# Expert feed-forward layer: the weights, not the tokens, held in the TensorE array

## The chip, the cores and the metric

The kernel runs on one core of a Trainium2 chip. The metric is device time in microseconds (us), lower is better. A run of the kernel before took 1444.42 us (median of three, 1442.44 to 1445.25). A profile of one execution gives for each engine what it did and when: TensorE (PE for matmuls, PEld for its loads of the stationary operand), VectorE (DVE), ScalarE (ACT), GpSimd (POOL) and SyncE (SP, whose queue issues the large loads).

## The reference

A two-layer decoder trunk on 256 tokens of 1024 channels, in float32. Each layer has a token mixer and a feed-forward part; the second layer's feed-forward part is a mixture of experts, and it alone is changed:

```
logits = h @ w_router                      # h: RMS-normed, 256 x 1024; 8 experts
top_vals, top_idx = top_k(logits, 2)       # each token goes to two experts
gates = softmax(top_vals)
for each expert e, on the tokens sent to it:
    y = (silu(x @ w_gate[e]) * (x @ w_up[e])) @ w_down[e]    # 1024 -> 3584 -> 1024
out[token] += gate * y
```

All eight experts together have 3 x 8 x 1024 x 3584 weights, 352 MB in float32, and every one is read once. With these inputs no expert gets more than 87 tokens.

## The kernel before, in words

A TensorE matmul holds a stationary operand (`lhsT`, up to 128 columns) in the array and streams a moving operand (`rhs`) past it; the result has one row per stationary column and lands in PSUM. A float32 matmul of the program is carried out as two load-and-stream pairs, so the profile counts two matmuls and two loads for each. The array can be used as four tiles of 32 columns each, which hold different operands and stream at the same time; which tile is meant is set by the output's start partition (0, 32, 64 or 96).

Tokens are gathered per expert (`fetch`, L969): a one-hot matrix of up to 96 columns (`CAP`) picks an expert's tokens out of `hn` by a matmul and leaves them in `xe`, channels on partitions. Tokens are the stationary operand. In `lanes` (L992 to L1003) the 96 tokens fill three of the four 32-column tiles, and 512 columns of the weights stream past (L998); the fourth tile takes the first 32 tokens of the next 512 weight columns (L999). The other 64 tokens of those columns are done in a second PSUM bank with 256 weight columns at a time (L1003). So each slice of 128 input channels and 1024 weight columns (a "k-step" below) takes two rounds of 512 columns and two of 256, four tiles at once, the pairs of passes counted.

`mm_in` runs eight k-steps for the gate or the up projection of 1024 hidden channels, `mm_down` four for half of that. A step `s` of the main loop (28 in all) is: gate, the rest of a finished expert if there is one, `turn`, the gather for a coming expert, up, and two `mm_down` for the step before. `turn` (L1030) transposes the 96 x 1024 hidden activations, since they come out with tokens on partitions and have to go in with channels there. `scales` (L983) fetches the gates and the norm factors per token, which `swi` and `y_evac` apply as per-partition scalars. `back` (L1070) and `scatter` (L1085) put a finished expert's output back to its tokens by one-hot matmuls and add it to `xt`.

TensorE's order is written out by hand in this stage. The weights come through a ring of nine 2 MB buffers: `Stream.done` (L216) issues the next load on SP's queue when the matmuls on a buffer have ended, so the loads run up to nine buffers ahead. At the end one branch (L1256) skips code for experts with more than `CAP` tokens.

Of the kernel before, what the change touches and what calls it, by code (L numbers as in the profile page):

```python
# [15 lines left out]
P = 128  # L16
T = 256
# [15 lines left out]
CAP = 96  # L33
# [4 lines left out]
def hybrid_decoder(  # L38
# [810 lines left out]
    hn = big.tile([P, 2, D], F32, tag="x3", name="hn")  # L849
    lps = bank("C")  # L850
# [33 lines left out]
    def sm2(name):  # L884
# [25 lines left out]
                             op0=OP.mult, op1=OP.add)  # L910
    region.close()


    io = moe.tile([P, 2, P], F32, name="io", bufs=1)
    for b, c0, n, pat, base in ((0, 0, 96, [[1, 96]], 0), (0, 96, 32, [[1, 32]], 0), (1, 0, 128, [[0, 2], [1, 64]], 32)):
        POOL.iota(io[:, b, c0:c0 + n], pattern=pat, base=base - BIG, channel_multiplier=0,
                  allow_small_or_imprecise_dtypes=True)
    lane = moe.tile([P, 3], F32, name="lane", bufs=1)
    DVE.memset(lane, 0.0)
    DVE.memset(lane[96:128, 0:1], 1.0)  # L920
    DVE.memset(lane[0:64, 1:2], 1.0)
    DVE.memset(lane[64:128, 2:3], 1.0)

    def onehot(scol, base, tag):
        g = moe.tile([P, 2, P], F32, tag=tag, name=tag, bufs=1)
        for t in range(2):
            DVE.tensor_scalar(g[:, t], base, scol(t), None, op0=OP.is_equal)
        return g
# [5 lines left out]
    def gates():  # L934
        ss = sm(2, "ss")
        for t in range(2):
            sq = big.tile([P, D], F32, tag="x2", name="sqt")
            ACT.activation(sq, xt[:, t], AF.Square, accum_out=ss[:, t:t + 1])
        r = rstd_from(ss, 2, 1.0 / D, "rstd")
# [27 lines left out]

    def fetch(e):

        g1 = onehot(lambda t: slot[:, t, e:e + 1], io[:, 0], "G1")  # L970
        g2 = onehot(lambda t: slot[:, t, e:e + 1], io[:, 1], "G2")
        xe = moe.tile([P, KD, CAP], F32, tag="xe", name="xe")
        for n in range(2):
            ps = bank("C")[:, 0:4 * CAP].rearrange("p (j l) -> p j l", j=4)
            for j in range(4):
                c = 4 * n + j
                for t in range(2):
                    PE.matmul(ps[:, j], lhsT=hn[:, t, c * P:(c + 1) * P], rhs=g1[:, t, 0:CAP],
                              start=(j == 0 and t == 0), stop=(t == 1), skip_group_check=True)
            (DVE.tensor_copy if n else ACT.copy)(xe[:, 4 * n:4 * n + 4], ps)  # L980
        return dict(e=e, x=xe, g1=g1, g2=g2)

    def scales(st):  # L983
        ps = bank("C")
        for b, g in enumerate((st["g1"], st["g2"])):
            for t in range(2):
                PE.matmul(ps[:, 2 * b:2 * b + 2], lhsT=g[:, t], rhs=gr[:, t, st["e"]], start=(t == 0), stop=(t == 1),
                          skip_group_check=True)
        gs = moe.tile([P, 4], F32, tag="gs", name="gs", bufs=3)
        DVE.tensor_copy(gs, ps[:, 0:4])  # L990
        st["gs"] = gs

    def lanes(b1, b2, l0, l1, w, start, stop, banks=(0, 1)):

        kw = dict(start=start, stop=stop, skip_group_check=True)
        if 0 in banks:
            for t in range(3):
                PE.matmul(b1[32 * t:32 * t + 32, :], lhsT=l0(t), rhs=w[:, 0:512], **kw)  # L998
            PE.matmul(b1[96:128, :], lhsT=l1(0), rhs=w[:, 512:1024], **kw)  # L999
        if 1 in banks:  # L1000
            for i in range(4):
                q = slice(512 + 256 * (i // 2), 768 + 256 * (i // 2))
                PE.matmul(b2[32 * i:32 * i + 32, 0:256], lhsT=l1(1 + i % 2), rhs=w[:, q], **kw)  # L1003

    def mm_in(nm, s, sts):
        b1, b2 = bank("A"), bank("A")
        x0, x1 = sts[0]["x"], sts[1]["x"]
        for k in range(KD):
            u = MU[nm, s, k - k % 4]
            w = ws.direct(u)[:, k % 4]  # L1010
            lanes(b1, b2, lambda t: x0[:, k, 32 * t:32 * t + 32], lambda t: x1[:, k, 32 * t:32 * t + 32],
                  w, k == 0, k == KD - 1)
            if k % 4 == 3:
                ws.done(u)
        return b1, b2

    def swi(sts, bg, bu):
        a = big.tile([P, 2, 768], F32, tag="x0", name="act")
        sg, pr = a[:, 0], a[:, 1]
        if sts[0] is sts[1]:  # L1020
            r1 = sts[0]["gs"][:, 1:2]
        else:
            r1 = moe.tile([P, 1], F32, tag="r1", name="r1")
            DVE.tensor_copy(r1[0:96], sts[0]["gs"][0:96, 1:2])
            DVE.tensor_copy(r1[96:128], sts[1]["gs"][96:128, 1:2])
        for b, q, r in ((0, slice(0, 512), r1), (1, slice(512, 768), sts[1]["gs"][:, 3:4])):
            n = q.stop - q.start
            ACT.activation(sg[:, q], bg[b][:, 0:n], AF.Silu, scale=r)
            DVE.scalar_tensor_tensor(pr[:, q], bu[b][:, 0:n], r, sg[:, q], op0=OP.mult, op1=OP.mult)  # L1029
        return pr  # L1030

    def turn(pr):
        ht = moe.tile([P, 6, P], F32, tag="ht", name="ht", bufs=1)
        for n, (f0, nf) in enumerate(((0, 4), (4, 2))):
            ps = bank("C")
            for f in range(nf):
                tp(ps[:, f * P:(f + 1) * P], pr[:, (f0 + f) * P:(f0 + f + 1) * P])
            (DVE.tensor_copy if n else ACT.copy)(ht[:, f0:f0 + nf], ps[:, 0:nf * P].rearrange("p (f l) -> p f l", f=nf))  # L1038
        return ht

    def hidden(ht, h, f):
        def of(t):
            if h == 0:
                return ht[:, f, 32 * t:32 * t + 32]
            if t == 0:
                return ht[:, f, 96:128]
            q = 64 * (f // 2) + 32 * (t - 1)
            return ht[:, 4 + f % 2, q:q + 32]
        return of

    def mm_down(q, ht, psd, banks=(0, 1)):
        u = MU["d", q]
        c = half_of(q)[1]
        for f in range(4):
            of = hidden(ht, q % 2, f)
            lanes(psd[0], psd[1], of, of, ws.direct(u)[:, f], c == 0 and f == 0, c == HCH - 1 and f == 3, banks)
        if 1 in banks:
            ws.done(u)

    def y_evac(st, psd, banks=(0, 1)):  # L1060
        if 0 in banks:
            st["y"] = big.tile([P, 2, 768], F32R, tag="x2", name="y")
        y = st["y"]
        for b, q in ((0, slice(0, 512)), (1, slice(512, 768))):
            if b in banks:
                ps, g = psd[b][:, 0:q.stop - q.start], st["gs"][:, 2 * b:2 * b + 1]
                ACT.activation(y[:, 0, q], ps, AF.Copy, scale=g)  # L1067
                DVE.scalar_tensor_tensor(y[:, 1, q], ps, g, y[:, 0, q].bitcast(F32), op0=OP.mult, op1=OP.subtract)  # L1068

    def back(st):  # L1070

        e = st["e"]
        ps = bank("C")
        for b in range(2):
            g = onehot(lambda t: slot[:, t, e:e + 1], io[:, b], f"G{b + 1}")
            for t in range(2):
                tp(ps[:, (2 * b + t) * P:(2 * b + t + 1) * P], g[:, t])
        s = moe.tile([P, 4, T], F32R, tag="S", name="S", bufs=1)
        ACT.copy(s[:, 0], ps[:, 0:T])
        for n in range(3):  # L1080
            ACT.activation(s[:, 1 + n], ps[:, 0:T] if n == 0 else ps[:, T:2 * T], AF.Copy, scale=lane[:, n:n + 1])  # L1081
        st["s"] = s

    def scatter(st, t, v):
        ps = bank("C")  # L1085
        s, y = st["s"], st["y"]
        q = slice(t * P, (t + 1) * P)
        if v == 0:
            for i in range(2):
                PE.matmul(ps, lhsT=s[0:96, 0, q], rhs=y[0:96, i, 0:512], start=(i == 0), stop=(i == 1))  # L1090
        else:
            kw = dict(skip_group_check=True)
            for i in range(2):
                PE.matmul(ps, lhsT=s[:, 1, q], rhs=y[:, i, 0:512], start=(i == 0), stop=False, **kw)  # L1094
            for n in range(2):
                for i in range(2):
                    PE.matmul(ps[:, 256 * n:256 * n + 256], lhsT=s[:, 2 + n, q], rhs=y[:, i, 512:768],  # L1097
                              start=False, stop=(i == 1), **kw)
        DVE.tensor_tensor(xt[:, t, v * 512:(v + 1) * 512], xt[:, t, v * 512:(v + 1) * 512], ps, op=OP.add)  # L1099
# [5 lines left out]
    ht = pr = None  # L1105
    whole = []

    def down_of(q):
# [3 lines left out]
        mm_down(q, ht, psd[e])  # L1112
# [4 lines left out]
    for s in range(NS):  # L1117
# [3 lines left out]
        if s == 0:  # L1121
            gates()
            scales(st[0])
# [168 lines left out]
```

## Time and profile before

| what | before |
|---|---|
| runs, median (range) | 1444.42 us (1442.44 to 1445.25) |
| profiled execution, its time / its span | 1444.4 us / 1442.6 us |
| PE busy, matmuls | 1390.0 us (96%), 14,642 |
| PEld busy, loads of the stationary operand | 828.1 us, 14,642 |
| DVE / ACT busy | 431.1 us (30%) / 286.1 us (20%) |
| moved by DMA | 423.91 MB, mean 294 GB/s |
| granted TensorE clock | 0.994 of full |

The profiled execution takes 1.8 us more than its span from the first to the last instruction. A busy PE only says that some matmul was under way; how many columns stream at that time is read from the pitch at which matmuls begin. The first 452 us hold both mixers and the dense feed-forward part, which the change does not touch; the expert layer follows, and the last 15 us are the final norm and the store.

### The profile page before, as it was taken

How to read it: one execution, taken by the hardware profiler on the slowest of the kernel's cores; microseconds unless marked ns; L12 is line 12 of the kernel's file. 1: busy time of each engine (PE TensorE's matmuls, PEld its weight loads, DVE VectorE, ACT ScalarE, POOL GpSimd, SP SyncE). 2: the span in 40 equal slices, each digit the busy share in tenths (PEclk: the TensorE clock that was granted, in tenths of full speed). 3: DMA queues.
4: the chain of work that ended last, by engine and by line, in shares of the span. 5: the costliest groups of instructions: out<-in, count | busy, mean ns of one | idle time of the engine just before them, and what ended most of it. 6: DMA issues, size and time to landing. Idle time of an engine off the chain costs nothing. (4 is left out here: it accounts for less than half of the span.)

```text
span 1442.6 us, 31733 instructions
## 1 busy us (share of the span) xinstructions
PE 1390.0 (96%) x14642; PEld 828.1 (57%) x14642; DVE 431.1 (30%) x933; ACT 286.1 (20%) x486; POOL 12.2 (1%) x27
## 2 busy tenths in 40 slices
PE   5999999999999999999999999999999999999995
PEld 4997999999976444444444444444444444444442
DVE  4997756568973000010010011010001001000102
ACT  4752444446712000000000010010001001000102
POOL 3000000000000000000000000000000000000000
PEclk9999999999999999999999999999999999999998
DMA  8653655553519999989998998999899999999830
GB/s 198 219 176 121 201 177 188 195 192 100 209 40 402 408 395 404 403 337 344 388 340 337 394 395 331 348 391 330 340 397 380 347 340 365 351 352 400 345 146 32
DMA packets 143264, 423.91 MB, mean 294 GB/s; under 512 B 4590, under 2 KB 33493, under 8 KB 143124
## 3 DMA queue, kind: packets, MB, share of 16 engines
q1 hardware_dynamic: 142420, 421.09, 77.8%
q0 software_dynamic: 688, 0.72, 0.6%
q8 instruction: 117, 1.92, 0.5%
q14 instruction: 23, 0.19, 0.0%
q10 hardware_dynamic: 16, 0.00, 0.0%
HBM read 420.74 MB, written 1.05 MB: 292 GB/s over the span
## 5 line engine op out<-in xcount | busy, mean ns | idle before, releaser
L998 PE MATMUL psA<-raw,xe 128*32 128x512 f32 x2688 | 464.2, 593 | 0.0
L999 PE MATMUL psA<-raw,xe 128*32 128x512 f32 x896 | 458.2, 593 | 0.0
L1003 PE MATMUL psA<-raw,xe 128*32 128x256 f32 x3584 | 275.4, 379 | 0.0
L1003 PEld LDWEIGHTS psA<-raw,xe 128*32 128x32 f32 x3584 | 116.3, 110 | 268.2 <-issue 268.2
L998 PE MATMUL psB<-raw,ht 128*32 128x512 f32 x1344 | 231.2, 592 | 0.0
L999 PE MATMUL psB<-raw,ht 128*32 128x512 f32 x448 | 228.3, 592 | 0.0
L407 PE MATMUL psB<-xh,whi 128*128 128x256 f32 x608 | 173.1, 285 | 0.0
L409 PE MATMUL psB<-xh,wlo 128*128 128x256 f32 x608 | 172.5, 284 | 0.0
L408 PE MATMUL psB<-xl,whi 128*128 128x256 f32 x608 | 172.2, 283 | 0.0
L234 DVE TENSOR_TENSOR wlo<-raw,whi 128x1024 fp32r<-128x1024 f32 x110 | 134.0, 1223 | 58.7 <-ACT whi L233 58.6
L998 PEld LDWEIGHTS psA<-raw,xe 128*32 128x32 f32 x2688 | 107.6, 110 | 75.7 <-PE psC L331 2.2
L1038 ACT COPY ht<-psC 128x512 f32<-128x512 f32 x28 | 16.4, 587 | 670.0 <-issue 412.9
L233 ACT CAST whi<-raw 128x1024 fp32r<-128x1024 f32 x110 | 114.7, 1048 | 113.2 <-PE psB L408 51.9
L1003 PE MATMUL psB<-raw,ht 128*32 128x256 f32 x1792 | 137.2, 379 | 0.0
L1038 DVE COPY ht<-psC 128x256 f32<-128x256 f32 x28 | 11.9, 425 | 416.4 <-PE psC L331 416.4
L1003 PEld LDWEIGHTS psB<-raw,ht 128*32 128x32 f32 x1792 | 58.1, 110 | 132.6 <-issue 132.1
L407 PEld LDWEIGHTS psB<-xh,whi 128*128 128x128 f32 x608 | 116.6, 192 | 0.7 <-issue 0.7
L409 PEld LDWEIGHTS psB<-xh,wlo 128*128 128x128 f32 x608 | 116.5, 192 | 0.2
L408 PEld LDWEIGHTS psB<-xl,whi 128*128 128x128 f32 x608 | 116.5, 192 | 0.0
L1029 DVE SCALAR_TENSOR_TENSOR act<-psA,gs,act 128x256 f32<-128x256 f32 (+1 forms) x52 | 29.3, 603 | 227.3 <-PE psA L999 227.3
L999 PEld LDWEIGHTS psA<-raw,xe 128*32 128x32 f32 x896 | 96.2, 110 | 0.0
L998 PEld LDWEIGHTS psB<-raw,ht 128*32 128x32 f32 x1344 | 55.1, 110 | 39.8 <-issue 2.0
(280 smaller groups left out, 1299.6 us busy)
## 6 DMA issues: line engine op xcount, KB each, us to landing
raw<-in_moe_w_down_dram SPq DMA_DIRECT2D x52, 2048.0 KB, 11.4
raw<-in_moe_w_gate_dram SPq DMA_DIRECT2D x48, 2048.0 KB, 9.6
raw<-in_moe_w_up_dram SPq DMA_DIRECT2D x46, 2048.0 KB, 11.2
raw<-in_w_in_dram SPq DMA_DIRECT2D x9, 2048.0 KB, 14.0
raw<-in_moe_w_gate_dram SPq DMA_DIRECT2D x16, 1024.0 KB, 6.7
raw<-in_moe_w_up_dram SPq DMA_DIRECT2D x16, 1024.0 KB, 10.8
raw<-in_ffn_w_gate_dram SPq DMA_DIRECT2D x11, 1024.0 KB, 5.4
raw<-in_ffn_w_up_dram SPq DMA_DIRECT2D x11, 1024.0 KB, 7.9
```

The lines of the kernel that those rows point to most:

```text
L233: ACT.copy(hi, raw)
L234: DVE.tensor_tensor(lo, raw, hi.bitcast(F32), op=OP.subtract)
L407: PE.matmul(ps, lhsT=hi, rhs=xh, start=start, stop=False, **kw)
L408: PE.matmul(ps, lhsT=hi, rhs=xl, start=False, stop=False, **kw)
L409: PE.matmul(ps, lhsT=lo, rhs=xh, start=False, stop=stop, **kw)
L998: PE.matmul(b1[32 * t:32 * t + 32, :], lhsT=l0(t), rhs=w[:, 0:512], **kw)
L999: PE.matmul(b1[96:128, :], lhsT=l1(0), rhs=w[:, 512:1024], **kw)
L1003: PE.matmul(b2[32 * i:32 * i + 32, 0:256], lhsT=l1(1 + i % 2), rhs=w[:, q], **kw)
L1029: DVE.scalar_tensor_tensor(pr[:, q], bu[b][:, 0:n], r, sg[:, q], op0=OP.mult, op1=OP.mult)
L1038: (DVE.tensor_copy if n else ACT.copy)(ht[:, f0:f0 + nf], ps[:, 0:nf * P].rearrange("p (f l) -> p f l", f=nf))
```

## The change

The operands of the expert matmuls swap places. 32 columns of the weights are now the stationary operand of each tile, so four tiles hold 128 weight columns, and the expert's 88 gathered token columns stream past all four (`blocks`). Outputs come with hidden channels on partitions, which is the layout that the down projection takes as its moving operand; `turn`, `hidden` and `scales` are gone. `CAP` is 88. The norm factor per token can no longer be a per-partition scalar, so it is folded into the gather's one-hot matrix, for which it has to be known before the first gather (the squares move into `route`, the reciprocal root ahead of `fetch`). The down projection's result also has channels on partitions; it is copied out and transposed once per expert (`y_turn`), and the scatter becomes two matmuls per block.

```
-CAP = 96
+CAP = 88
...
+            for t in range(2):
+                ACT.activation(sqt, xt[:, t, q], AF.Square, accum_out=ssq2[:, c // 4, t:t + 1])
...
+    ss = sm(2, "ss")
+    DVE.tensor_tensor(ss, ssq2[:, 0], ssq2[:, 1], op=OP.add)
+    r_ffn = rstd_from(ss, 2, 1.0 / D, "rstd")
...
-        g1 = onehot(lambda t: slot[:, t, e:e + 1], io[:, 0], "G1")
-        g2 = onehot(lambda t: slot[:, t, e:e + 1], io[:, 1], "G2")
+        g = onehot(lambda t: slot[:, t, e:e + 1], io, "G1", lambda t: r_ffn[:, t:t + 1])
...
+    def blocks(ps, w, rhs, nk, n0, nb, start, stop):
+        for b in range(nb):
+            for k in range(nk):
+                for j in range(4):
+                    c = n0 + b * P + 32 * j
+                    PE.matmul(ps[32 * j:32 * j + 32, b * CAP:(b + 1) * CAP], lhsT=w(k)[:, c:c + 32], rhs=rhs(k),
+                              start=start and b == 0 and k == 0, stop=stop and k == nk - 1, skip_group_check=True)
     def mm_in(nm, s, sts):
...
+        for k0 in (0, 4):
+            u = MU[nm, s, k0]
+            raw = ws.direct(u)
+            for h in range(2):
+                x = sts[h]["x"]
+                blocks(banks[h], lambda k: raw[:, k], lambda k: x[:, k0 + k], 4, 512 * h, 4, k0 == 0, k0 == 4)
+            ws.done(u)
...
+    def swi(bg, bu):
+        sg = big.tile([P, 2, 4 * CAP], F32, tag="x0", name="sg")
+        ht = moe.tile([P, 2, 4, CAP], F32, tag="ht", name="ht")
+        for h in range(2):
+            ACT.activation(sg[:, h], bg[h][:, 0:4 * CAP], AF.Silu)
+            DVE.tensor_tensor(ht[:, h].rearrange("p f l -> p (f l)"), bu[h][:, 0:4 * CAP], sg[:, h], op=OP.mult)
...
+        for v in banks:
+            blocks(psd[v], lambda k: raw[:, k], lambda k: ht[:, q % 2, k], 4, 512 * v, 4, c == 0, c == HCH - 1)
...
+    def prepare(st):
+        for t in range(2):
+            tp(ps[0:CAP, t * P:(t + 1) * P], g[:, t])
+        for t in range(2):
+            PE.matmul(ps[0:CAP, T:T + 1], lhsT=g[:, t], rhs=gr[:, t, e, 0:1], start=(t == 0), stop=(t == 1), ...)
...
+    def y_turn(st, v):
+        for b in range(4):
+            tp(ps[0:CAP, b * P:(b + 1) * P], st["yt"][:, v, b])
+        ACT.activation(y[0:CAP, 0, q], ps[0:CAP], AF.Copy, scale=g)
+        DVE.scalar_tensor_tensor(y[0:CAP, 1, q], ps[0:CAP], g, y[0:CAP, 0, q].bitcast(F32), ...)
...
-        if s:
-            ht = turn(pr)
```

On TensorE, where a gate projection ends and the step's `turn` and up projection follow, the order before is this (`raw` is a weight buffer, `xe` the gathered tokens, `ident,act` the transposes of `turn`; sizes are those of the output):

```order
L998 MATMUL psA<-raw,xe 32x512 x3
L999 MATMUL psA<-raw,xe 32x512
L1003 MATMUL psA<-raw,xe 32x256 x4
L331 MATMUL psC<-ident,act 128x128 x6
L998 MATMUL psA<-raw,xe 32x512 x3
L999 MATMUL psA<-raw,xe 32x512
L1003 MATMUL psA<-raw,xe 32x256 x4
```

And now, from a gate projection on to the end of an expert and its way back to its tokens (`yt` is the down projection's result before its transposes):

```order
L987 MATMUL psA<-xe,raw 32x88 x512
L987 MATMUL psB<-ht,raw 32x88 x128
L987 MATMUL psA<-xe,raw 32x88 x256
L987 MATMUL psB<-ht,raw 32x88 x128
L331 MATMUL psC<-ident,G_8864 88x128 x2
L1026 MATMUL psC<-gr,G_8864 88x1 x2
L331 MATMUL psC<-ident,yt 88x128 x8
L1057 MATMUL psC<-y,S 128x512 x8
```

A gate or up projection was 64 matmuls of the program in eight k-steps of eight; it is 256 of 88 columns each, a half of a down projection 128. The transposes `ident,act` between gate and up are gone, the transposes `ident,yt` are new, once per expert.

On DVE, between the routing and the first gather, there stood the choice of the experts' slots and then at once the one-hot matrix. Now it is this (`slot` is the choice, `ss` the sum of squares, `rstdv` the first step of the norm factor, `m` and `mv` belong to the gates, `G_8864` to the way back of the first expert):

```order
L913 SCALAR_TENSOR_TENSOR slot<-sel,psC 128x16
L916 TENSOR_TENSOR ss<-ssq_4693 128x2
L943 TENSOR_SCALAR m_5111<-rk 128x16
L943 TENSOR_SCALAR m_5112<-rk 128x16
L439 TENSOR_SCALAR rstdv<-ss 128x2
L944 TENSOR_TENSOR mv<-m_5111,lg 128x16
L927 TENSOR_SCALAR G_8864<-io,slot 128x88
```

From `ss` on, 22 small DVE instructions now stand between the slots and the matrix of the first gather (`G_4824`, L929), for which TensorE waits.

## Rows read from the trace of the kernel before

**Rows 1.** Page, part 1: busy us (share of the span) xinstructions
```profile
PE 1390.0 (96%) x14642; PEld 828.1 (57%) x14642; DVE 431.1 (30%) x933; ACT 286.1 (20%) x486; POOL 12.2 (1%) x27
```

**Rows 2.** Stretches: length, busy (x) PE, PEld, DVE, ACT, POOL, clock, DMA share, GB/s
```profile
452.00:1427.00 975.00, 959.43 (x11362) 417.14 (x11361) 94.70 (x230) 70.24 (x145) 0.00 (x0) 1.00 0.91 351
500.00:1300.00 800.00, 787.53 (x9322) 345.50 (x9318) 74.64 (x176) 54.60 (x112) 0.00 (x0) 1.00 0.95 364
1425.30:1426.90 1.60, 1.60 (x33) 0.94 (x32) 1.60 (x4) 1.21 (x4) 0.00 (x0) 1.00 0.04 10
```

**Rows 3.** Groups of TensorE in the expert layer: count, busy us, mean ns, idle before
```profile
L998 PE MATMUL psA<-raw,xe 128*32 128x512 f32 x2688 | 464.2, 593 | 0.0
...
L1003 PE MATMUL psA<-raw,xe 128*32 128x256 f32 x3584 | 275.4, 379 | 0.0
```

**Rows 4.** DMA by queue, 500 to 1300 us: packets, MB, share of 16 engines
```profile
q1 hardware_dynamic: 81485, 290.10, 94.5%
...
q8 instruction: 73, 1.20, 0.6%
```

**Rows 5.** Chain that ended last, 1360 to 1371 us: start, us, what
```profile
1360.46 0.43 PE psA L1003 x8
...
1370.78 0.43 PE psB L1003 x8
```

**Rows 6.** Timeline, TensorE, after other work: start us, us, engine line, instructions
```profile
906.23 0.63 PE L998 MATMUL psA<-raw,xe 128*32 128x512 f32 x3
...
906.68 0.60 PE L998 MATMUL psA<-raw,xe 128*32 128x512 f32 x3
...
907.11 0.40 PE L1003 MATMUL psA<-raw,xe 128*32 128x256 f32 x4
```

**Rows 7.** Timeline, TensorE, in the middle of a projection
```profile
910.12 0.60 PE L998 MATMUL psA<-raw,xe 128*32 128x512 f32 x3
910.12 0.12 PEld L998 LDWEIGHTS psA<-raw,xe 128*32 128x32 f32 x3
910.14 0.59 PE L999 MATMUL psA<-raw,xe 128*32 128x512 f32 x1
910.14 0.11 PEld L999 LDWEIGHTS psA<-raw,xe 128*32 128x32 f32 x1
```

**Rows 8.** DMA, 1429 to 1434 us, in 40 slices of 0.125 us
```profile
DMA  0000000060000000000000000000000000005000
...
q8 instruction: 2, 0.03, 3.0%
```

**Rows 9.** Timeline, TensorE, a turn between two projections
```profile
484.25 0.61 PE L1003 MATMUL psA<-raw,xe 128*32 128x256 f32 x8
...
484.80 0.87 PE L331 MATMUL psC<-ident,act 128*128 128x128 f32 x6
...
485.60 0.63 PE L998 MATMUL psA<-raw,xe 128*32 128x512 f32 x3
```

**Rows 10.** Timeline, TensorE, a gather and its scales
```profile
518.07 3.81 PE L978 MATMUL psC<-G,hn 128*128 128x96 f32 x32 [0.50 <-ACT ht L1038]
...
521.72 0.98 PE L987 MATMUL psC<-gr,G 128*128 128x2 f32 x8
...
522.63 0.63 PE L998 MATMUL psA<-raw,xe 128*32 128x512 f32 x3
```

**Rows 11.** Timeline, slots and first gather; last two rows: around an expert's way back
```profile
447.72 0.16 DVE L909 SCALAR_TENSOR_TENSOR slot<-sel,psC 128x16 f32<-128x16 f32 x1
...
447.98 0.87 DVE L927 TENSOR_SCALAR G<-io,slot 128x128 f32<-128x128 f32 x4
...
448.42 3.78 PE L978 MATMUL psC<-G,hn 128*128 128x96 f32 x32 [0.98 <-DVE G L927]
...
616.99 0.61 PE L1003 MATMUL psB<-raw,ht 128*32 128x256 f32 x8
...
622.79 0.60 PE L331 MATMUL psC<-ident,act 128*128 128x128 f32 x4
```

More of the change, by code (lines that the diff above doesn't have):

```diff
@@ L849, in hybrid_decoder @@
     hn = big.tile([P, 2, D], F32, tag="x3", name="hn")
+    sqt = big.tile([P, 512], F32, tag="x4", name="sqt")
+    ssq2 = moe.tile([P, 2, 2], F32, name="ssq2", bufs=1)
     lps = bank("C")
@@ L910, in hybrid_decoder, with onehot @@
                              op0=OP.mult, op1=OP.add)
+    ss = sm(2, "ss")
+    DVE.tensor_tensor(ss, ssq2[:, 0], ssq2[:, 1], op=OP.add)
+    r_ffn = rstd_from(ss, 2, 1.0 / D, "rstd")
     region.close()
[L914 to L924, printed above, removed]
+    io = moe.tile([P, CAP], F32, name="io", bufs=1)
+    POOL.iota(io, pattern=[[1, CAP]], base=-BIG, channel_multiplier=0, allow_small_or_imprecise_dtypes=True)
+    def onehot(scol, base, tag, scale=None):
         g = moe.tile([P, 2, P], F32, tag=tag, name=tag, bufs=1)
+        n = base.shape[-1]
         for t in range(2):
-            DVE.tensor_scalar(g[:, t], base, scol(t), None, op0=OP.is_equal)
-        return g
+            if scale is None:
+                DVE.tensor_scalar(g[:, t, 0:n], base, scol(t), None, op0=OP.is_equal)
+            else:
+                DVE.tensor_scalar(g[:, t, 0:n], base, scol(t), scale(t), op0=OP.is_equal, op1=OP.mult)
+        return g[:, :, 0:n]
     gr = moe.tile([P, 2, E, 2], F32, name="gr", bufs=1)
@@ L934, in gates @@
     def gates():
[L935 to L939, printed above, removed]
+        r = r_ffn
         DVE.tensor_copy(gr[:, :, :, 1], r[:, :, None].to_broadcast([P, 2, E]))
@@ L977, in fetch @@
                 for t in range(2):
-                    PE.matmul(ps[:, j], lhsT=hn[:, t, c * P:(c + 1) * P], rhs=g1[:, t, 0:CAP],
+                    PE.matmul(ps[:, j], lhsT=hn[:, t, c * P:(c + 1) * P], rhs=g[:, t],
                               start=(j == 0 and t == 0), stop=(t == 1), skip_group_check=True)
             (DVE.tensor_copy if n else ACT.copy)(xe[:, 4 * n:4 * n + 4], ps)
[L981 to L1003, printed above, removed]
@@ L1005, in mm_in @@
-    def mm_in(nm, s, sts):
[L1006 to L1038, printed above, removed]
-        return ht
[L1041 to L1049, printed above, removed]
+        return dict(e=e, x=xe)
@@ new lines, in blocks @@
+    def blocks(ps, w, rhs, nk, n0, nb, start, stop):
[5 more added lines that the diff above has]
+                              start=start and b == 0 and k == 0, stop=stop and k == nk - 1, skip_group_check=True)
+    def mm_in(nm, s, sts):
+        banks = [bank("A"), bank("A")]
+        for k0 in (0, 4):
[5 more added lines that the diff above has]
+            ws.done(u)
+        return banks
@@ L1053, in mm_down @@
         c = half_of(q)[1]
-        for f in range(4):
-            of = hidden(ht, q % 2, f)
-            lanes(psd[0], psd[1], of, of, ws.direct(u)[:, f], c == 0 and f == 0, c == HCH - 1 and f == 3, banks)
+        raw = ws.direct(u)
+        for v in banks:
+            blocks(psd[v], lambda k: raw[:, k], lambda k: ht[:, q % 2, k], 4, 512 * v, 4, c == 0, c == HCH - 1)
         if 1 in banks:
             ws.done(u)
+    def prepare(st):
+        e = st["e"]
+        g = onehot(lambda t: slot[:, t, e:e + 1], io, "G2")
+        ps = bank("C")
+        for t in range(2):
+            tp(ps[0:CAP, t * P:(t + 1) * P], g[:, t])
+        for t in range(2):
+            PE.matmul(ps[0:CAP, T:T + 1], lhsT=g[:, t], rhs=gr[:, t, e, 0:1], start=(t == 0), stop=(t == 1),
+                      skip_group_check=True)
+        s = moe.tile([P, T], F32R, tag="S", name="S", bufs=1)
+        ACT.copy(s[0:CAP], ps[0:CAP, 0:T])
+        gs = moe.tile([P, 1], F32, tag="gs", name="gs")
+        DVE.tensor_copy(gs[0:CAP], ps[0:CAP, T:T + 1])
+        st["s"], st["gs"] = s, gs
@@ L1060, in y_evac @@
     def y_evac(st, psd, banks=(0, 1)):
         if 0 in banks:
[L1062 to L1068, printed above, removed]
@@ L1070, in back @@
-    def back(st):
-        e = st["e"]
-        ps = bank("C")
[L1074 to L1082, printed above, removed]
+            st["yt"] = moe.tile([P, 2, 4, CAP], F32, tag="yt", name="yt", bufs=1)
@@ new lines, in y_evac @@
+        for v in banks:
+            (DVE.tensor_copy if v else ACT.copy)(st["yt"][:, v].rearrange("p b l -> p (b l)"), psd[v][:, 0:4 * CAP])
+    def y_turn(st, v):
+        if v == 0:
+            st["y"] = big.tile([P, 2, D], F32R, tag="x2", name="y")
+        ps = bank("C")
+        for b in range(4):
+            tp(ps[0:CAP, b * P:(b + 1) * P], st["yt"][:, v, b])
+        y, g = st["y"], st["gs"][0:CAP]
+        q = slice(512 * v, 512 * v + 512)
+        ACT.activation(y[0:CAP, 0, q], ps[0:CAP], AF.Copy, scale=g)
+        DVE.scalar_tensor_tensor(y[0:CAP, 1, q], ps[0:CAP], g, y[0:CAP, 0, q].bitcast(F32),
+                                 op0=OP.mult, op1=OP.subtract)
@@ L1084, in scatter @@
     def scatter(st, t, v):
         ps = bank("C")
[L1086 to L1098, printed above, removed]
@@ L1099, in scatter @@
-        DVE.tensor_tensor(xt[:, t, v * 512:(v + 1) * 512], xt[:, t, v * 512:(v + 1) * 512], ps, op=OP.add)
+        q = slice(512 * v, 512 * v + 512)
+        for i in range(2):
+            PE.matmul(ps, lhsT=st["s"][0:CAP, t * P:(t + 1) * P], rhs=st["y"][0:CAP, i, q],
+                      start=(i == 0), stop=(i == 1))
+        DVE.tensor_tensor(xt[:, t, q], xt[:, t, q], ps, op=OP.add)
     pe = ExitStack()
@@ L1104, in hybrid_decoder @@
     psd = {}
-    ht = pr = None
+    hts = {}
     whole = []
@@ L1122, in hybrid_decoder @@
             gates()
-            scales(st[0])
         if straddles(s - 2):
@@ L1127, in hybrid_decoder @@
             e = whole.pop()
-            back(st[e])
-            for t in range(2):
-                for v in range(2):
+            prepare(st[e])
+            for v in range(2):
+                y_turn(st[e], v)
+            for v in range(2):
+                for t in range(2):
                     scatter(st[e], t, v)
             st.pop(e)
-        if s:
-            ht = turn(pr)
         n = half_of(2 * s + 3)[0] if s + 1 < NS else e1
@@ L1137, in hybrid_decoder @@
             st[n] = fetch(n)
-            scales(st[n])
         bu = mm_in("u", s, sts)
-        pr = swi(sts, bg, bu)
+        hts[s] = swi(bg, bu)
         if s:
@@ L1144, in hybrid_decoder @@
                 down_of(2 * s - 1)
-    ht = turn(pr)
-    back(st[E - 1])
-    mm_down(2 * NS - 2, ht, psd[E - 1])
+    prepare(st[E - 1])
+    mm_down(2 * NS - 2, hts[NS - 1], psd[E - 1])
     wfin = rb_pool.tile([P, D], F32, tag="raw_b", name="wfin")
@@ L1178, in last_half @@
         if t == 0:
-            mm_down(2 * NS - 1, ht, psd[E - 1], (v,))
+            mm_down(2 * NS - 1, hts[NS - 1], psd[E - 1], (v,))
             y_evac(st[E - 1], psd[E - 1], (v,))
+            y_turn(st[E - 1], v)
         scatter(st[E - 1], t, v)
```

4 lines of the change are left out of this document (2 added, 2 removed).

## The prediction

> **What bounds the kernel now.** I read the busy shares first, then stretches, then the costliest groups, the chain that ended last, and timelines of single rounds. TensorE is busy 96% of the span [rows 1], and in the expert layer, 452 to 1427 us, 959 of 975 us [rows 2]. DVE and ACT are busy there a tenth of the time or less, so no copy bounds this stage; the reader should see that no idle time stands before the expert matmuls [rows 3], so that they wait for no weights. DMA is close behind: 94.5% of 16 engines in 500 to 1300 us [rows 4].
>
> How fast TensorE works is in the pitch. Eight k-steps take from 1360.46 to 1370.78 us [rows 5], 1.29 us each. Within one, a 512-column round takes 0.43 us (906.68 to 907.11 [rows 6]). [...] The layer has 28 x 24 = 672 k-steps: 867 us.
>
> One more number matters: in that stretch TensorE starts 9322 + 9318 = 18,640 instructions in 800 us [rows 2], one per 43 ns. The queue named "instruction" moves 73 packets meanwhile [rows 4], one per 255 instructions and per 11 us: TensorE's program is itself fetched by DMA, in packets of 255 or 256. Nothing bounds there now.
>
> **The change, the streaming.** A k-step's 1024 weight columns become 8 blocks of 4 x 32, in two passes: 16 rounds of 88 columns instead of four longer ones. 672 x 16 = 10,752 rounds. If columns still set the pace, a round is 88 x 0.833 + 2.5 = 75.8 ns, all of them 815 us: 52 us less.
>
> **The change, the instructions.** A round is four loads and four matmuls as before, but there are four times as many: 10,752 x 8 = 86,016 instead of 21,504. At 75.8 ns a round this is one instruction per 9.5 ns. No row shows such a pace held. Two bounds: eight instructions start within some 0.02 us [rows 7], 3 ns each, but those had long been waiting in TensorE's queue; the densest run, 65 in 1.6 us [rows 2], third row,, is 25 ns each, and still paced by columns.
>
> The fetch bounds it more closely. 86,016 instructions are 337 packets; at 9.5 ns a packet's worth lasts 2.4 us. One packet occupies its engine for 0.006 x 16 x 800 / 73 = 1.05 us, so if several could be under way, the fetch would keep up. But the end of the trace shows how packets come. After the last scatter TensorE takes the branch over the unused code. One packet comes at 1430.06 us, the next at 1433.56, with idle DMA engines between [rows 8]: 3.5 us a packet (each moving for 0.030 x 16 x 5 / 2 = 1.2 us), and no second one asked for along with the first. If a packet is asked for only when the one before is entered, it cannot take less than that round trip. I take the row as it is: 337 x 3.5 = 1180 us, 313 us more than the 867. A packet can cost more, since it shares engines with 2 MB loads that occupy all of them for 5.5 us (290.10 MB in 800 x 0.945 us [rows 4]); a quarter of that waited on average gives 4.8 us and 1618 us. It may cost less, since part of the 3.5 us is the branch; at 2.64 us per packet, 10.3 ns per instruction, the gains below are just used up.
>
> [...]
>
> **The change, the rest of TensorE's work.** `turn` goes: from 484.25 + 0.43 = 484.68 (when the next round could start) to 485.60 us [rows 9], 0.92 us, 28 times: -25.8 us. What hid behind it is nothing, as TensorE starts the next round at once. `scales` goes: 521.72 to 522.63 [rows 10], 0.91 us, 8 times: -7.3 us. An expert's way back took TensorE from the last round's end at 616.99 + 0.43 = 617.42 us to 622.79 [rows 11], 5.4 us. The new one has two transposes and four small products (0.11 us each, the pitch of rows 10), eight transposes (0.9 us), then ACT's scaled copy and DVE's second half (0.7 us each, my estimate, above the 0.4 us that DVE's four instructions of the third row of [rows 2] take on the mean) and four scatters that alternate with DVE's additions in two banks: I count 6.0 us, 0.6 x 7 = +4 us. The last expert pays two more copies and transposes, +2.4 us. Gathers stay at 32 pairs of 0.11 us.
>
> The norm factor ahead of the first gather adds 22 DVE instructions of 0.16 to 0.2 us: the matrix that began 0.26 us after the slots [rows 11] begins some 4.3 us later, TensorE waits for it with the gate projection queued behind, and nothing hides that: +4.3 us. ACT's four squares end before DVE asks for their sum. The loads' queue is not moved past anything; buffers come free as the matmuls go. Together: -25.8 - 7.3 + 4 + 2.4 + 4.3 = -22 us.
>
> **Sum.** Against the profiled execution's 1444.4 us (1442.6 span and 1.8 around it; the median of the runs is the same): 1444.4 + 313 - 22 = 1735 us.
>
> **Rivals.** (1) Columns set the pace, because more than one packet is fetched ahead. Then 1444.4 - 52 - 22 = 1370 us, faster by 5%. [...] Against it: rows 8. The weights would nearly bind as well: 352 MB in some 895 us is 393 GB/s, and the stage shows 384 GB/s per full share of the engines (290.10 MB / 800 us / 0.945), so up to 20 us of this gain may go to waiting for weights, 1390 us. The mechanism decides at 2.64 us per packet: below it the kernel is faster, above it slower.
>
> (2) TensorE's front end starts instructions at a fixed pace of its own. Between the 10.3 ns at which nothing changes and the 25 ns of the densest run the middle is 17.6 ns: 1514 us for the tiles, 1444.4 + 647 - 22 = 2069 us. No row excludes it, none asks for it.
>
> (3) The four tiles' loads run one after another. 128 columns pair at 0.11 us (the gather, 32 pairs in 3.6 us [rows 10]), so four loads of 32 in a row would take 0.11 us and pace the round: 10,752 x 0.111 = 1193 us, 1748 us in all. Against it: after other work, when no load could run ahead, the first round takes 0.45 us instead of 0.43 (906.23 to 906.68 [rows 6]), so four loads cost 0.02 us, not 0.11. [...]
>
> (4) The time per packet falls near 2.64 us and the two cancel: about 1445 us.
>
> **How the numbers follow.** Forecast (packets one at a time, 2.7 to 4.8 us each, 1465 to 2150 us) 0.62; rival 1 0.26; rival 2 0.06; rival 3 0.03; rival 4 0.03. A change of 0.2% (3 us) is what runs of this kernel can tell from none. Slower 0.71, same 0.03, faster 0.26. Of the forecast's own range about 1500 to 2100 us is likely. The range for 8 in 10 has to take in rival 1 for the most part and leaves out its faster part and the slowest packets: 1360 to 2150 us.
>
> **What would show it.** If right, the 88-column rounds come in runs at about 76 ns, broken by idle time of TensorE after every 255 or so instructions, with no DMA of weights, DVE or ACT as releaser, one instruction packet per gap, over 330 packets more than now, and weights at under 320 GB/s. Rival 1 shows the same packets 2.4 us apart and a share of DMA near 1; rival 2 an even pitch of 8 x its pace without gaps; rival 3 a pitch of 0.11 us. The way back of an expert should take about 6 us, and the first gather start 4 us later after the slots. The forecast is wrong if packets follow one another in less than 2.6 us.

## The result, and the profile after

The changed kernel takes 2170.91 us (median of four runs, 2167.02 to 2175.04), the kernel before in the same comparison 1443.51 us: a ratio of 1.504, 95% interval 1.500 to 1.508. Slower was forecast, but by 290 us, not by 727, and the time lies just above the range.

Page of the changed kernel, part 1 (busy us, share of the span, instructions), then the two groups of expert matmuls; the number behind the bar's second part is the idle time just ahead of them and what ended it:

```profile
PE 1575.1 (73%) x46682; PEld 1488.0 (69%) x46682; DVE 414.8 (19%) x870; ACT 265.3 (12%) x446; POOL 11.8 (1%) x25
...
L987 PE MATMUL psA<-xe,raw 128*32 128x88 f32 x28672 | 710.8, 267 | 355.4 <-issue 355.3
...
L987 PE MATMUL psB<-ht,raw 128*32 128x88 f32 x14336 | 369.9, 271 | 183.7 <-issue 183.5
```

Where [rows 1] had TensorE busy 96% and [rows 3] no idle time, it now stands idle 539 us (355.3 + 183.5) ahead of the expert matmuls, and what ended the idle time is "issue": nothing that the profile shows as work. The stretch of the expert layer (columns as in [rows 2]):

```profile
452.00:2150.00 1698.00, 1144.18 (x43301) 1076.62 (x43301) 75.00 (x153) 47.59 (x96) 0.00 (x0) 0.85 0.57 204
```

The granted clock is 0.85 there, and DMA is busy at only 0.57. So neither the weights nor full-speed columns bound the stage.

The chain that ended last, 1143 to 1167 us (start, us, what):

```profile
1143.00 1.07 PE psA L987 x57
1144.07 3.58 issue
1147.65 1.24 PE psA L987 x26
...
1149.03 4.94 PE psB L987 x226
1153.97 3.63 issue
1157.60 1.24 PE psB L987 x26
...
1158.99 5.07 PE psA L987 x225
1164.07 3.04 issue
1167.11 2.91 PE psA L987 x78
```

TensorE works off 256 matmuls and their 256 loads, two packets of instructions, stands still for 3 to 3.6 us, and goes on. The DMA view of the same stretch, 1143 to 1183 us, in slices of 1 us, shows what comes in between (first line: busy share in tenths, second: GB/s):

```profile
DMA  9950000889999000089999800069999910046999
GB/s 430 414 229 8 4 16 0 98 340 434 406 438 369 16 12 16 0 102 389 418 426 430 320 20 8 16 66 307 422 414 434 410 45 16 0 57 197 414 418 426
```

Each load of 2 MB is a block of five to seven slices at up to 438 GB/s, with DMA idle between two of them, and there is one load to a stall. The trace's packet starts are 1145.40, 1148.78, 1155.11, 1158.87, 1164.77 and 1168.17 us: 3.4 to 3.8 us apart, then 5.9 to 6.3. The second, the fourth and the sixth come alone (16 GB/s in the slices at 1148 and 1158); the first, the third and the fifth start in the last microsecond of a load. The whole stage looks like this: in the trace from 470 to 2050 us, ahead of a packet that comes more than 5.5 us after the last, 298 pieces of weights (4 KB each) start in the 3 us before it and 34 in the 3 us after it; with less than 4.2 us it is 4 before and 102 after (medians of 151 and 154 packets).

Packets in 500 to 1300 us (queue: packets, MB, share of 16 engines), to be compared with [rows 4]:

```profile
q1 hardware_dynamic: 45785, 165.13, 57.1%
q8 instruction: 158, 2.59, 1.3%
```

158 packets in 800 us are one per 5.06 us; before, there were 73. From the first expert round to the last it is 457.66 to 2154.71 us, 1697 us, or 336 packets at 5.05 us; before it was 452.13 to 1426.88, 975 us. That is +722 us; the first round comes 5.5 us later, the end after the last round is 1.3 us longer, and the span is 729 us longer.

### The profile page after: what moved, and what is told of

Its sections match the earlier page's. It is cut to its first block, busy times and chain, and to the rows that moved or that the text cites. A ratio compares the mean times of both kernels' runs of the same rounds, so it can differ in the third digit from the quotient of the medians.

```text
span 2171.7 us, 95639 instructions
## 1 busy us (share of the span) xinstructions
PE 1575.1 (73%) x46682; PEld 1488.0 (69%) x46682; DVE 414.8 (19%) x870; ACT 265.3 (12%) x446; POOL 11.8 (1%) x25
## 4 chain that ended last, share of the span: by engine, by line
PE 71%; issue 25%; DVE 2%; ACT 1%; DMA 1%; SPq 0%; ACTq 0%; DVEq 0%
PE psA L987 32%; PE psB L987 17%; PE psB L407 3%; PE psB L409 3%; PE psB L408 3%; PE psA L691 2%; PE psC L976 2%; PE psA L408 1%; PE psA L409 1%; PE psA L407 1%; PE psC L1057 1%; DMA raw<-in_w_in_dram 1%; PE psC L331 1%; DVE y L1050 0%; ACT y L1049 0%
## 5 line engine op out<-in xcount | busy, mean ns | idle before, releaser
L987 PE MATMUL psA<-xe,raw 128*32 128x88 f32 x28672 | 710.8, 267 | 355.4 <-issue 355.3
L987 PEld LDWEIGHTS psA<-xe,raw 128*32 128x32 f32 x28672 | 674.2, 126 | 389.2 <-issue 386.8
L987 PE MATMUL psB<-ht,raw 128*32 128x88 f32 x14336 | 369.9, 271 | 183.7 <-issue 183.5
L987 PEld LDWEIGHTS psB<-ht,raw 128*32 128x32 f32 x14336 | 347.9, 128 | 201.0 <-issue 200.9
L691 PE MATMUL psA<-yf,raw 128*128 128x256 f32 x256 | 60.5, 391 | 5.4 <-ACT yf L731 3.0
L691 PEld LDWEIGHTS psA<-yf,raw 128*128 128x128 f32 x256 | 48.5, 195 | 13.0 <-ACT yf L731 3.5
L976 PE MATMUL psC<-G,hn 128*128 128x88 f32 x256 | 44.7, 354 | 8.7 <-issue 5.0
L538 DVE SCALAR_TENSOR_TENSOR conv<-gp,pc,conv 128x256 f32<-128x256 f32 x120 | 50.7, 475 | 0.0
L408 PE MATMUL psA<-al,whi 128*128 128x256 f32 x176 | 49.8, 283 | 0.0
L409 PE MATMUL psA<-ah,wlo 128*128 128x256 f32 x176 | 49.7, 282 | 0.0
```

What stands on the lines that cost most here:

```text
L408: PE.matmul(ps, lhsT=hi, rhs=xl, start=False, stop=False, **kw)
L409: PE.matmul(ps, lhsT=lo, rhs=xh, start=False, stop=stop, **kw)
L538: DVE.scalar_tensor_tensor(conv[:, c], src, w, conv[:, c], op0=OP.mult, op1=OP.add)
L691: PE.matmul(acc[j][:, a], lhsT=raw[:, k, w], rhs=yf[b][:, k], start=(b + k == 0 and a == 0), stop=(b + k == 4), skip_group_check=True)
L976: PE.matmul(ps[:, j], lhsT=hn[:, t, c * P:(c + 1) * P], rhs=g[:, t], start=(j == 0 and t == 0), stop=(t == 1), skip_group_check=True)
L987: PE.matmul(ps[32 * j:32 * j + 32, b * CAP:(b + 1) * CAP], lhsT=w(k)[:, c:c + 32], rhs=rhs(k), start=start and b == 0 and k == 0, stop=sto ...
```

## The experiments

Where no interval stands, it is one run; the kernel before took 1443.59, 1444.41 and 1444.24 us (runs 1 to 4, 5 to 8 and 9 to 11).

**1. The count alone, in the old layout.** Tokens stay stationary, each matmul is cut in four.

```
-            for t in range(3):
-                PE.matmul(b1[32 * t:32 * t + 32, :], lhsT=l0(t), rhs=w[:, 0:512], **kw)
...
+            for m in range(4):
+                a, z = 128 * m, 128 * (m + 1)
+                kw["start"] = start and m == 0
+                for t in range(3):
+                    PE.matmul(b1[32 * t:32 * t + 32, a:z], lhsT=l0(t), rhs=w[:, a:z], **kw)
...
```

> The kernel before, tokens still stationary and in the same layout, but each 512-column matmul of the experts cut into four of 128 and each 256-column one into four of 64: the same columns (1536 a k-step), four times the TensorE instructions (86,016, as many as in the changed kernel). If the count of instructions and their fetch set the time, a packet of 256 costs the 5.05 us of the changed kernel: 336 x 5.05 = 1697 us in place of 867, about 2270 us, with gaps of TensorE at every second packet. If it is the weights as stationary operand, their loads or the 88-column rounds, the columns set the pace as before: about 1445 us.

Measured: 2180.91 us. Queue and stretch, 600 to 1400 us:

```profile
q8 instruction: 159, 2.61, 1.3%
...
600.00:1400.00 800.00, 565.24 (x20240) 531.35 (x20236) 44.98 (x100) 32.12 (x66) 0.00 (x0) 0.87 0.58 208
```

159 packets in 800 us, one per 5.03 us, as in the changed kernel. Neither the stationary weights nor the new layout make it slow: four times the instructions do, in the old kernel too. The expected 2270 us are 89 too many: the price of 5.05 us is a mean over the whole stage and already holds the layer's other work, which the sum then adds once more.

**2. Half the columns.**

```
-                    PE.matmul(ps[..., b * CAP:(b + 1) * CAP], lhsT=w(k)[:, c:c + 32], rhs=rhs(k),
+                    PE.matmul(ps[..., b * CAP:b * CAP + 44], lhsT=w(k)[:, c:c + 32], rhs=rhs(k)[:, 0:44],
...
```

> The changed kernel with 44 instead of 88 columns streamed in every expert matmul (half of the tokens left out): the same instructions, half the columns. Fetch in pairs: packets still start 3.4 to 3.6 us and then some 5.2 to 6.3 us apart (the second stretch holds the execution of one packet's worth, 2.4 us at 88 columns and full clock, 1.3 to 2.4 at 44), so 1880 to 2150 us. Columns at a reduced clock: the expert rounds halve, weights bind at about 400 GB/s, about 1400 us. A fixed pace of some 19.7 ns per instruction: 2170 us without change and without gaps.

Measured: 2173.58 us, the changed kernel's time. Half of the streaming is gone and nothing is gained, not even the part that the expectation for a fetch in pairs had (1880 to 2150 us):

```profile
q8 instruction: 158, 2.59, 1.3%
...
600.00:1400.00 800.00, 403.33 (x20083) 367.83 (x20079) 33.45 (x79) 18.61 (x49) 0.00 (x0) 0.63 0.58 209
```

Busy time falls, packets stay at 5.06 us: what a packet's worth takes to execute is no part of the longer interval. The granted clock is down to 0.63 and that costs nothing either: the reduced clock is not what makes the kernel slow. A fixed pace per instruction, which also gives 2170 us, would leave no gaps, and the chain above shows them.

**3. No weight traffic.**

```
+                if u >= N_T1 + 24:
+                    self.raw[u] = self.kept[u % 4]
+                    self.loaded += 1
+                    continue
...
```

Instead of a load, one of the last four buffers is used again.

> The changed kernel without the expert weights' loads after the first 24 of 84 buffers' worth of the layer (the last four buffers are used again and again, so the result leaves those weights out): the same TensorE instructions, DMA almost idle. Fetch as a round trip of its own: packets keep their 3.5 us and about 6.3 us, time within 5% of 2171 us. Fetch slowed by the weight traffic: packets follow faster, from 5.05 towards the 2.4 us that a packet's worth executes in, 1400 to 1800 us.

Measured: 1827.46 us. The first of the two expectations fails; the second holds in its direction, with a time 27 us above its range. Queues in 600 to 1400 us, and a stretch of the timeline (start us, us, what; in brackets the idle time before):

```profile
q8 instruction: 206, 3.38, 1.8%
q1 hardware_dynamic: 1185, 4.66, 1.6%
```

```profile
1001.52 2.63 PE L994 MATMUL psA<-xe,raw 128*32 128x88 f32 x128 [0.84 <-issue]
1005.26 2.63 PE L994 MATMUL psA<-xe,raw 128*32 128x88 f32 x128 [1.11 <-issue]
1009.28 2.63 PE L994 MATMUL psA<-xe,raw 128*32 128x88 f32 x128 [1.39 <-issue]
1012.75 2.63 PE L994 MATMUL psA<-xe,raw 128*32 128x88 f32 x128 [0.84 <-issue]
```

Packets now mostly come 3.5 to 4.0 us after the last (206 in 800 us: one per 3.88). Six of them take 6.7 to 8.6 us, five of these at an expert's way back; the alternation is gone, and in the stretch shown TensorE stops after each packet. Two things follow. The round trip of 3.5 us that [rows 8] showed is near what a packet costs alone, and packets come one at a time even with DMA idle. And the alternation is made by the loads. The 128 matmuls and 128 loads run in 2.4 us, 9.4 ns per instruction at a granted clock of 0.98: TensorE can take instructions at that pace.

**4. Half the instructions, the same columns.**

```
-                for j in range(4):
-                    c = n0 + b * P + 32 * j
-                    PE.matmul(ps[32 * j:32 * j + 32, b * CAP:(b + 1) * CAP], lhsT=w(k)[:, c:c + 32], rhs=rhs(k),
+                for j in range(2):
+                    c = n0 + b * P + 64 * j
+                    PE.matmul(ps[64 * j:64 * j + 64, b * CAP:(b + 1) * CAP], lhsT=w(k)[:, c:c + 64], rhs=rhs(k),
```

> The changed kernel on two tiles of 64 weight columns instead of four of 32: the same 10,752 rounds of 88 columns, half the instructions (43,008), 19 ns each at column pace. Fetch in pairs with no running ahead: 2 x 4.85 us of execution and one stall of 3.5 us per pair, 13.2 us x 84 = 1109 us, about 1660 us; if TensorE's queue hides the round trip, 815 us, about 1370 us; I expect some of both, 1450 to 1660 us. A fixed pace of 19.7 ns per instruction: 847 us, about 1400 us, with no gaps. Loads of 64 columns that pace the round: some 0.11 us a round, about 1750 us.

Measured: 1495.86 us, in the expected 1450 to 1660. It is 675 us faster than the changed kernel, with the same streamed columns and the same layout of the results; what differs is the count, and that one load fills 64 columns instead of 32. Queue in 600 to 1400 us, and the timeline:

```profile
q8 instruction: 134, 2.20, 1.1%
```

```profile
577.08 5.07 PE L987 MATMUL psB<-ht,raw 128*64 128x88 f32 x128 [0.58 <-issue]
583.00 1.66 PE L987 MATMUL psB<-ht,raw 128*64 128x88 f32 x38 [0.85 <-issue]
```

Packets are 5.97 us apart on the mean, execution takes 4.85 of it. DMA is now nearly full (346 GB/s in the stretch, against 208 in the changed kernel), so most packets should meet a load. TensorE's idle time is still put down to "issue" (76 us of the 800) and not to a load of weights.

**5. Both: half the instructions and no weight traffic.** The edits of 3 and 4.

> Two tiles of 64 columns, and no loads of expert weights after the first 24 buffers (the rest is computed from the last four buffers). If a packet costs the longer of its execution (4.85 us here) and its round trip (3.5 to 3.9 us without weight traffic), the round trip is hidden, rounds of 88 columns run without gaps: 815 us, about 1370 us. If TensorE can't keep a pace of 19 ns per instruction, or loads of 64 columns pace the rounds: about 1450 to 1500 us, as with the weights loaded.

Measured: 1387.46 us. Timeline:

```profile
1002.48 19.58 PE L994 MATMUL psA<-xe,raw 128*64 128x88 f32 x512
```

512 matmuls, four packets, in one piece. So the rule holds from both sides: a packet costs the longer of its execution (4.85 us) and its round trip (mostly 3.5 to 4.0 us without loads, about 6 when it meets a load of 2 MB).

**6. Smaller descriptors.** Each 2 MB load in two halves of 512 columns, issued together.

```
+                elif u >= N_T1:
+                    w = d["n"] // 2
+                    for n in range(2):
+                        nc.sync.dma_start(t[:, :, n * w:(n + 1) * w], d["src"][:, :, n * w:(n + 1) * w])
...
```

> Two tiles of 64 columns, all weights loaded, but each 2 MB load issued as two halves of 512 columns, so that a DMA descriptor moves 2 KB (84 ns) instead of 4 KB (159 ns). If a packet waits behind a fixed number of descriptors in its DMA engine, its 2.7 us of extra wait halves, the round trip falls from about 6.1 to about 4.9 us, level with execution: 1380 to 1430 us, faster than the kernel before. If it waits for a share of bytes or for the whole load, nothing changes: 1490 us, or more, as 2 KB moves 6% slower.

Measured: 1516.99 us, 1.051 of before (1.048 to 1.055). The faster expectation fails, the other one (1490 us or more) holds. Queue in 600 to 1400 us:

```profile
q8 instruction: 131, 2.15, 1.1%
```

Packets are 6.1 us apart, where run 4 had 5.97, though the weights now come in 134,504 pieces of 2 KB (267.13 MB) instead of 75,420 for 274.23 MB. They do not wait for a fixed number of descriptors.

**7. A quarter of the instructions, one tile of 128 columns.**

```
+                for j in range(1):
+                    c = n0 + b * P + 128 * j
+                    PE.matmul(ps[128 * j:128 * j + 128, b * CAP:(b + 1) * CAP], lhsT=w(k)[:, c:c + 128], rhs=rhs(k),
```

> One tile of 128 weight columns: the same 10,752 rounds of 88 columns, two instructions each, 21,504 as in the kernel before, 84 packets. Their fetch (6.2 us a packet, 521 us) is hidden in any case. If loads of 128 columns hide behind the stream, rounds at 76 ns give about 1370 us, faster than before; if load and stream pace a round at the 0.114 us of the gather's pairs, 10,752 x 0.114 = 1226 us, about 1780 us, with no gaps.

Measured: 2873.94 us, 1.991 of before (1.988 to 1.995), outside both expectations. Stretches from the gather on, then 600 to 1400 us:

```profile
440.00:448.00 8.00, 4.34 (x41) 4.28 (x40) 6.08 (x36) 4.35 (x9) 0.00 (x0) 1.00 1.02 409
448.00:452.00 4.00, 4.00 (x24) 4.00 (x24) 0.90 (x7) 1.57 (x3) 0.00 (x0) 0.59 1.03 410
452.00:456.00 4.00, 4.00 (x21) 4.00 (x21) 0.99 (x3) 0.37 (x1) 0.00 (x0) 0.50 1.03 408
```

```profile
600.00:1400.00 800.00, 798.56 (x3726) 794.16 (x3726) 23.08 (x47) 15.01 (x31) 0.00 (x0) 0.50 0.41 147
```

3726 rounds in 800 us, 0.215 us each, without gaps: the fetch is hidden, as expected. But the clock fell to 0.50 after TensorE had stood idle 3.66 us ahead of the first gather, and it did not come back. At this clock the 88 columns alone should take 2 x 0.075 = 0.15 us (an estimate from run 3's round at a clock of 0.98), so the load of 128 columns does not seem to hide behind the stream. The round is about twice the 0.114 us of the gather's pairs at full clock [rows 10]; what it would itself take at full clock was not measured.

**8. Loads held back, four at a time.**

```
+            f = self.freed if self.freed < N_T1 else N_T1 + (self.freed - N_T1) // 4 * 4
+            self.load_upto(f + self.limit)
```

> The changed kernel with the loads held back and issued four buffers at a time (8 MB, some 21 us of DMA), everything else the same. If a packet's wait depends on whether a load is under way (6.2 us against 3.5 to 3.9), the alternation of 3.5 and 6.3 us goes: runs of about three long intervals and four or five short ones, 4.8 us on average, 2080 to 2171 us. If packets come in pairs by themselves, the alternation stays with all its numbers.

Measured: 2155.71 us, with 161 packets in 600 to 1400 us and the alternation as it was. The time lies in the expected range and still says nothing, because the edit did not do what it should: in the DMA view the loads come one at a time as before (1100 to 1140 us):

```profile
DMA  0077999910067999930002789997000047999910
```

Why the edit did not hold them together is not shown.

**9. Loads of 512 KB, changed kernel.** Each quarter of a buffer is loaded again as soon as it is used up.

```
+                elif u >= N_T1:
+                    for k in range(0, d["k"], 1):
+                        nc.sync.dma_start(t[:, k:k + 1], d["src"][:, k:k + 1])
...
+        for k in range(nk):
+            for h in hs:
+                for b in range(4):
...
```

The buffer `t` is kept and not taken anew, and the input slice `k` is the outermost loop of the blocks.

> The changed kernel with each 2 MB load of expert weights issued as four of 512 KB, each as soon as the rows it replaces have been used (TensorE's blocks run with the input slice outermost for that): the same instructions and columns. If a packet waits for the load that is under way to end, it now waits at most 1.3 us instead of some 5: intervals of 3.5 and 6.3 us give way to 3.5 to 4.8, about 4.2 on average, 337 x 4.2 = 1415 us for the tiles, about 1880 us. If the wait depends on the mean DMA load alone, or the alternation is the fetch's own, nothing changes: 2150 to 2180 us.

Measured: 1957.55 us, 213 us less; 181 packets in 600 to 1400 us, one per 4.42 us:

```profile
q8 instruction: 181, 2.97, 1.5%
```

The direction is that of a packet that waits for the load under way: the same bytes per packet, in pieces of a quarter, cost it less, although DMA is busier than in the changed kernel (0.76 against 0.58). The price was right too: clear of gathers and ways back, packets start 4.2 us apart in the trace (218 of them). The 1880 us were too hopeful because they add nothing for the layer's other work.

**10. The same on two tiles.**

The edits of 4 and 9.

> Two tiles of 64 columns with the same loads of 512 KB. If a packet waits for the load under way, its round trip falls from 6.1 to 3.5 to 4.8 us, at or below the 4.85 us that a packet's worth executes in, and rounds run almost without gaps: 1385 to 1430 us, faster than the kernel before. If the wait depends on the mean DMA load (0.93 of full share here), no change: about 1495 us.

Measured: 1463.92 us, 1.015 of before (1.011 to 1.020): 32 us better than with 2 MB loads, and short of the forecast. 138 packets in 800 us, one per 5.80 us. DMA is at 357 GB/s and 0.95 of its share; that a packet therefore meets piece after piece would explain the shortfall, and is not shown. Waits of TensorE in 600 to 1400 us (what for: us, times, longest):

```profile
PE psA L999 <- issue: 26.3, 35, 1.8
PE psB L999 <- issue: 23.5, 31, 1.4
```

50 us of 800 are left; with 2 MB loads they were 76 (49.5 + 26.7). Run 5 shows what is still missing: at 1387 us the fetch is hidden.

**11. The control to 10: its order of blocks, 2 MB loads.**

The edit of 4 and the loops of 9.

> The control to the run with 512 KB loads on two tiles: TensorE's blocks in the same order (input slice outermost), loads of 2 MB as in the first run on two tiles. If only the size and the spacing of the loads matter, about 1495 us; if the order of the blocks does it, the time of the run with 512 KB loads.

Measured: 1493.42 us. On two tiles the order of the blocks is worth nothing measurable; the loads did it. Whether their size or their spacing counts is open, as each quarter is also issued by itself when it is used up, and two halves issued together gained nothing (run 6); for run 9 the order alone was not tried. No run that loads all the weights beats the kernel before.

## Why the prediction was right and wrong

**Right: what bounds it.** The streaming was priced right: within a burst of run 3 a packet's worth takes 2.4 us, 9.4 ns an instruction, for 9.5 predicted. The 0.833 ns a column and 2.5 ns a round that the 75.8 ns and rival 1's 52 us are made of, no run shows: in the trace of the kernel before, rounds of 512 columns start 429 ns apart and rounds of 256 columns 216 ns (medians), 0.84 ns a column in both, and the sum of 75.8 ns is met by run 5, whose 256 rounds from 1002.48 to 1021.89 us take 75.8 ns each. That the fetch and not the columns decides, that packets come one at a time and that the round trip alone is 3.5 to 4.0 us is confirmed by runs 1, 2 and 3. Rival 1 (several packets ahead) falls with run 3. Rival 2 named a time nearer to the result, 2069 us, but not its cause: there is no even pace, and at 9.4 ns TensorE keeps up. Rival 3 falls with the 75 ns of a round in a burst. Two signs were off: TensorE stops after two packets and not after each, and "over 330 packets more than now" was a miscount, as the layer had 90 packets before and has 339 now.

**Wrong: the size of one term.** The step that failed is "I take the row as it is: 337 x 3.5 = 1180 us". [Rows 8] are from the end of the program, where DMA is idle; in the expert layer every packet shares the engines with the weights. The mean over the layer is 5.05 us, other work included. Clear of gathers and ways back, packets start 4.9 us apart in the trace (238 of them, 15 us behind such work and 5 us ahead of it; 4.86 to 4.96 with other limits).

The text priced that wait as a case of its own, by a random meeting of packet and load, and then did not take it. Yet meeting comes in a fixed beat here: a buffer of 2 MB is exactly two packets' worth of matmuls (128 matmuls of the program, 512 instructions), so one load comes to every two packets. In the stretch above TensorE goes over to the next buffer at 1148.54 us, and SP issues the load into the one used up (timeline of SP: start us, us, what; the second of the two follows at 1159 us):

```profile
1149.07 10.33 SPq L200 DMA_DIRECT2D raw<-in_moe_w_gate_dram  x2
```

That is 0.3 us behind the start of a packet. DMA is busy with the load until about 1156 us, and the next packet starts in its last microsecond, 6.3 us after the one before. The packet after that finds DMA idle: 3.8 us. Half of the sum of 3.5 and 6.3 is 4.9. By the means over a stretch (5.06 and 3.88), the loads cost 1.2 us per packet. Run 3 left out 144 of the layer's 168 loads (its expectation says 84 buffers in all, a slip): 288 packets x 1.18 = 340 us, and it is 344 us faster than the changed kernel.

**A slip in the range.** The forecast's case of 4.8 us per packet gives 1444.4 + (1618 - 867) - 22 = 2173 us by the prediction's own sum, and not the 2150 at which its range ends. (A quarter of 5.5 us on top of 3.5 is 4.9, moreover, not 4.8.) That 2173 lies so near the measured time is partly luck: with 4.9 us the sum is 2207, and terms that were carried too high take it back.

**Partly wrong: the way the terms add.** With 5.05 us the sum would be 2257 us, but that mean already holds the layer's other work. Gathers, transposes and ways back were carried as terms of their own beside the packets, in full. With 4.9 us the sum is 1444.4 + (337 x 4.9 - 867) - 22 = 2207 us, 36 too many. In the stage 1697 - 336 x 4.9 = 51 us are left for all such work, where the kernel before had 975 - 867 = 108 and the prediction keeps 79 (108 - 25.8 - 7.3 + 4). So some of it hides while the next packet is on its way, and some does not; the 51 us move by about 17 with the 0.05 us that the price is uncertain by. What `turn` and `scales` are worth beside the fetch is not settled: run 1, which still has them and the old way back, takes 10 us more than the changed kernel.

**The small terms.** Timeline from the slots to the first round (start us, us, what):

```profile
447.25 0.16 DVE L913 SCALAR_TENSOR_TENSOR slot<-sel,psC 128x16 f32<-128x16 f32 x1
...
450.16 0.56 DVE L929 TENSOR_SCALAR G<-io,slot,rstd 128x88 f32<-128x88 f32 x2
```

```profile
450.63 7.10 PE L976 MATMUL psC<-G,hn 128*128 128x88 f32 x32 [3.66 <-DVE G L929]
457.66 6.71 PE L987 MATMUL psA<-xe,raw 128*32 128x88 f32 x258
```

The matrix starts 2.91 us after the slots instead of 0.26 [rows 11], 2.65 us later and not 4.3, as many of the 22 instructions overlap. But the gather then takes 7.1 us instead of 3.8, which no step foresaw: TensorE had stood idle 3.66 us (0.98 us in the kernel before), and its granted clock is 0.50 in that gather (1.00 in the kernel before, 448.4 to 452.2 us):

```profile
450.60:457.70 7.10, 7.07 (x36) 6.94 (x38) 1.15 (x9) 1.94 (x3) 0.00 (x0) 0.50 1.03 410
```

First round: +5.5 us in all. The way back of an expert, from the first transpose to the next round:

```profile
761.33 0.66 PE L331 MATMUL psC<-ident,G 128*88 128x128 f32 x2
...
764.90 4.13 PE L1057 MATMUL psC<-y,S 88*128 88x512 f32 x8 [0.70 <-DVE y L1050]
...
768.96 6.23 PE L987 MATMUL psA<-xe,raw 128*32 128x88 f32 x256
```

7.6 us, for 6.0 forecast and 5.4 before. It is the longest of the seven, which take 5.7 to 7.6 us with the waits for packets in them; in run 3 they take 5.7 to 6.5. The end behind the last round is 1.3 us longer. The forecast had 2.4 us for two more copies and transposes, of which only one stands behind that round.

**Open.** That a packet waits for the end of the load under way rests on the starts in the trace and on runs 3, 5, 9 and 10 against 4, 6 and 11. How the DMA engines share their time between queues is not settled: run 6 excludes a fixed number of descriptors, run 9 a wait that goes by the mean DMA load alone, but run 10 fell short of what waiting for one piece of 512 KB would give. Loads in real bursts were not tried, as run 8 did not make them.

## What to carry to other kernels

Before you cut matmuls into more and narrower ones, divide the new time by the number of instructions / 256 and compare it with what a packet of instructions costs under the traffic of that very stage (here 3.5 to 4 us alone, about 6 when it meets a 2 MB load). A row from an idle stretch was here the lower bound of such a price, not its value (3.5 us against 4.9), and packets and loads that come at a fixed ratio (here two packets to a load) met in a fixed beat, not at random. A mean over a stage already holds its other work; a price from a stretch clear of that work does not, and then some of the work has to be added (here about 51 us, where 79 were carried).

## What was not expected of the hardware

TensorE's granted clock fell to 0.50 after 3.66 us of idling, and whether it rose again differed by what came next: with tiled rounds of 32 columns it did (0.75 in the 6.3 us after the changed kernel's first gather, 0.85 over its expert layer, 0.98 in 600 to 1400 us of run 3), with rounds of one 128-column load and an 88-column stream it stayed at 0.50 (452 to 500 and 600 to 1400 us of run 7), with TensorE busy 798.56 of 800 us in the second stretch. Why is open. And in run 3, 256 instructions were worked off in 2.4 us, at the columns' pace: at 9.4 ns each, TensorE showed no fixed time per instruction of its own; what held it up was their arrival.
